# A hybrid attention and recurrence layer on one core: the first loads and transposes reordered, and a sixth token tile turned by VectorE and DRAM

## The chip, the core and the metric

The kernel runs on one core of one Trainium2 chip. A core has TensorE (matrix products and transposes, into PSUM banks of 128 x 512 f32), VectorE, ScalarE, GpSimd, and SyncE, which issues most DMAs. Each engine works through its own instructions in order and waits on semaphores for the others. The metric is the time of one execution on the device, in microseconds (us); lower is better. All data is f32, and no product may lose f32 accuracy.

## What is computed

One layer on 1024 tokens of width 1024, with 16 learned meta tokens ahead of them:

```python
h = concatenate([meta, x])                       # 1040 x 1024
u = rmsnorm(h, g_pre_mix);  z = u @ w_in         # -> q | k | v | x_rec | y_rec
attn = sliding_window_attention_with_sinks(q, k, v, sinks)   # 8 heads, window 128
xr = causal_depthwise_conv(x_rec, conv_w, conv_b)
rec = gelu(y_rec) * rg_lru(xr, w_a, b_a, w_x, b_x, lru_lambda)
h = h + rmsnorm(concatenate([attn, rec]) @ w_out, g_post_mix)
u = rmsnorm(h, g_pre_ffn)
f = square(relu(u @ w_ff1)) @ w_ff2
out = (h + rmsnorm(f, g_post_ffn))[16:]
```

`rmsnorm(x, g)` is x times the inverse root of (mean of x squared + 1e-6), times g.

## The kernel before, in words

**Products.** Every operand is split into a high part (rounded to fp32r) and a low part (the rest), and each f32 product is three fp32r products: high x high, high x low, low x high (`mm3`, L123; `part`, L279, does one of the three over all eight chunks of the contraction). ScalarE makes high parts (`nc.scalar.copy` or `activation`), VectorE the low parts. The engines' order is set by a scheduler that runs through the program with its own estimate of times; `behind(name, ins)` (L106) adds an order without a semaphore, `chained(e, ins)` (L332) strings instructions of ScalarE (e = 0) or VectorE (e = 1) together in the order of the text, and `lut` (L81) does so for ScalarE's table functions.

**The head** (up to about 50 us). SyncE issues the loads: meta, token tiles x0 and x1 (128 x 1024 each), the gains g_pre_mix and g_pre_ffn, then the columns of w_in for the keys, values and the first queries, further token tiles in between. The tokens go through in four blocks, `ALL` (L288): 272 columns (meta, x0, x1), then three of 256. For a block, `normed` (L320) makes the rows u without the gain: the square's sum on ScalarE, the inverse root (for x0 and x1 with ScalarE's Sqrt and VectorE's reciprocal, `norm_first` L232 and `root_rstd` L195; for the others with GpSimd's add and power, `norm_rows` L251 and `rstd_of` L167), and the scaling of the rows on VectorE. `transposed` (L351) then turns each of the eight 128-column chunks on TensorE into a PSUM bank (tags `pt`, `o`, `s`, two banks each), from where ScalarE writes the high part times the gain g_mix (L117) and VectorE the low part (L118). While this goes on, TensorE runs products of zeros: `load` (L307), 18 before the first transposes and one behind each chunk of block 0 (L365). The cast of the keys' weights stands in two halves between ScalarE's first evictions (`key_casts`, L344 and L368). Block 0's products are written out by hand (L503 to L525): keys and values in three parts, while x2 and x3 are normed, then two pairs of query heads. Blocks 1 to 3 (L526 to L530) are straight. The squares of x4 and of later tiles stand where the scheduler puts them.

**The middle** (to about 246 us) is attention, the convolutions and the recurrence, with projections filled in between on TensorE. It ends with the mix `at` = [attention | recurrence], ready in halves of 512 tokens.

**The output projection** (about 246 to 313 us). For each of the eight tiles t of 128 tokens, `out_mm` (L1030) makes two PSUM banks of 512 columns; `out_norm` (L1048) squares them on ScalarE (L1055), takes the inverse root on GpSimd (L172, L176), multiplies by root and g_post_mix on VectorE (L1061), adds x (L1064), stores h to `out` and squares h (L1067). h lies in a buffer of tag `raw`, of which there are two, shared with the loads of the feed-forward weights. `out_scale` (L1074) then brings the normed row tile into columns, in one of two ways. For t < `MOVED` (five tiles), `u2_store` (L1010) multiplies h by root and g_pre_ffn on VectorE with a dealt order of columns (L1011: every fourth column together), turns blocks of 32 x 32 on VectorE (L1018), and stores the result to DRAM, from where `u2_read` (L1021) fetches it with tokens along the columns. For the others ScalarE (t = 7: VectorE) scales the rows (L1081, L1079), and `u2_tiles` (L1087) turns them in eight TensorE transposes (L1093), with eight evictions that multiply by g_ffn (L1110 and L1101).

**The feed-forward products** (313 us to the end) are two Strassen-like schemes, over W1 and W2. The first sums of the token operand are made by `t_sums` (L1246) as tiles 4 to 7 come in.

Of the kernel before, what the change touches and what calls it, by code (L numbers as in the profile page):

```python
# [9 lines left out]
F32 = mybir.dt.float32  # L10
# [27 lines left out]
def hybrid_layer(  # L38
# [30 lines left out]
    def f32(ap):  # L69
        return ap.bitcast(F32)  # L70
# [68 lines left out]
    make_identity(nc, ident)  # L139

    meta_t = slot("d", [NMETA, D])
    nc.sync.dma_start(meta_t, meta_tokens)
    xt = []

    def load_x(i):
# [5 lines left out]
    load_x(1)  # L151

    vmt = const.tile([P, P], F32, name="vmt")
    g_r = vmt[0:16, :]
    nc.sync.dma_start(g_r[0:8, :], g_pre_mix.rearrange("o (k p) -> (o k) p", p=P))
    nc.sync.dma_start(g_r[8:16, :], g_pre_ffn.rearrange("o (k p) -> (o k) p", p=P))

    gcol = const.tile([P, 16], F32, name="gcol")
    pg = bank("o")
    nc.tensor.transpose(pg[:, :16], g_r, ident[:16, :16])  # L160
    nc.vector.tensor_copy(gcol, pg[:, :16])
    g_mix_col, g_ffn_col = gcol[:, 0:8], gcol[:, 8:16]

    half_pow = const.tile([P, 1], F32, name="half_pow")
# [27 lines left out]

    load_root()

    def root_rstd(ssq, bias, n=P):  # L195
        sd = small.tile([P, 1], F32, name="sd", tag="sd")
        lut(sd[:n], ssq, AF.Sqrt, bias=bias)
        rs = small.tile([P, 1], F32, name="rs", tag="rs")
        nc.vector.reciprocal(rs[:n], sd[:n])
        return rs[:n]  # L200


    def load_cols(cols, tag="ws"):
# [28 lines left out]
    def norm_first(src, halves):  # L232

        xn = slot("d", [P, D])
        ss = [small.tile([P, 1], F32, name=f"hq{i}", tag=f"hq{i}") for i in range(2)]
        c = slice(0, 512 if halves else D)
        nc.scalar.activation(
            xn[:, c], src[:, c], AF.Square, scale=RMS_SC, accum_out=ss[0]
        )
# [6 lines left out]
        rs = root_rstd(ss[0], ss[1] if halves else eps_col)  # L246
        for c in (slice(0, 512), slice(512, D)):
            nc.vector.tensor_scalar(xn[:, c], src[:, c], rs, None, op0=ALU.mult)
        return xn

    def norm_rows(src, n, link=False):  # L251
        xn = slot("d", [P, D])
        ssq = small.tile([P, 1], F32, name="ssq", tag="ssq")
        ins = nc.scalar.activation(
            xn[:n], src, AF.Square, scale=RMS_SC, accum_out=ssq[:n]
        ).ins
        if link:
            chained(0, ins)
        rs = rstd_of([ssq[:n]], n)
        ins = nc.vector.tensor_scalar(xn[:n], src, rs, None, op0=ALU.mult).ins  # L260
        if link:
            chained(1, ins)
        return xn

    def project(w, pieces, sink, after=None):
# [33 lines left out]

    zeros = slot("ws", [P, 512], F32R)  # L300
    nc.vector.memset(f32(zeros), 0.0)

    flip = [0]

# [9 lines left out]
                behind(after, ins)  # L314
        return ins.name

    load(12, 512)
    load(6, 256)

    def normed(b):  # L320
        if b == 0:
            return [
                (norm_rows(meta_t[:NMETA], NMETA), NMETA),
                (norm_first(xt[0], True), P), (norm_first(xt[1], False), P),
            ]
        rows = [(xt[2 * b], P), (xt[2 * b + 1], P)]
        return [(norm_rows(s[:m], m), m) for s, m in rows]


    last = [None, None]  # L330
# [3 lines left out]
            behind(last[e], ins)  # L334
        last[e] = ins.name

    def high_w(raw, tag="ws", parts=None):
        hi, lo = pair(tag, [P, KC, P])
        if parts is None:
            chained(0, nc.scalar.copy(hi, raw).ins)  # L340
            return hi, lo
        for ks in (slice(0, KC // 2), slice(KC // 2, KC)):
            parts.append(
                lambda ks=ks: chained(0, nc.scalar.copy(hi[:, ks], raw[:, ks]).ins)  # L344
            )
        return hi, lo

    def low_w(w, raw):
# [2 lines left out]
    def transposed(b, xn, after=None):  # L351
        t0, n = ALL[b]
        for kc in range(KC):
            flip[0] += 1
            pt = bank(("pt", "o", "s")[flip[0] % 3])
            o = 0
            for s, m in xn:
                ins = nc.tensor.transpose(
                    pt[:, o : o + m], s[:m, kc * P : (kc + 1) * P], ident[:m, :m]
                )  # L360
                if after:
                    behind(after, ins.ins)
                o += m
            if b == 0:
                load(1, P, ins.ins.name)  # L365
            uh, ul = u[kc]
            if b == 0 and kc in (0, 1):
                key_casts.pop(0)()  # L368
# [4 lines left out]
            if b == 0:  # L373
                chained(0, high[0])
                chained(1, high[1])

    def fetch(cols, tag="raw", pieces=1):
        raw = slot(tag, [P, KC, P])
# [21 lines left out]
    rq1 = fetch([(Q_COL + HD, HD), (Q_COL + 5 * HD, HD)], "e")  # L400
    for i in range(4, 8):
        load_x(i)
    key_casts = []
    wk = high_w(rk, "b", key_casts)
    transposed(0, xn)
    low_w(wk, rk)
    wv = high_w(rv, "b")
    low_w(wv, rv)
    wq = high_w(rq)
    low_w(wq, rq)  # L410
    km = slot("ws", [P, 4, 2 * P], F32R)
    nc.gpsimd.memset(f32(km[:, 0:2, 0 : P - NMETA]), 0.0)
    nc.gpsimd.memset(f32(km[:, 2:4, :]), 0.0)
    nsink = const.tile([P, 8], F32, name="nsink")
    nc.sync.dma_start(nsink, attn_sinks[0].partition_broadcast(P))
    prm_r = slot("d", [8, 512])
    nc.sync.dma_start(prm_r[0:4, :], conv_w[0])
    for i, src in ((4, conv_b), (7, lru_lambda)):
        nc.sync.dma_start(prm_r[i : i + 1, :], src)

    for i, src in enumerate((b_a, b_x)):
        for s in range(2):
            nc.sync.dma_start(
                prm_r[5 + s : 6 + s, :].rearrange("o (c t k) -> t o c k", t=2, k=HD)[i ^ s],
                src.rearrange("o (c t k) -> t o c k", t=2, k=HD)[s],
            )

# [71 lines left out]
    for b in range(4):  # L499
# [3 lines left out]
        if b == 0:  # L503

            acc = [bank("acc"), bank("acc")]
            for a, w in zip(acc, (wk, wv)):
                part(a, w, piece, 0)
                part(a, w, piece, 1)
            xn = [(norm_rows(xt[2], P, True), P)]
            xn.append((norm_rows(xt[3], P, True), P))  # L510
            part(acc[0], wk, piece, 2)
            sink_k(acc[0][:, : piece[1]], *piece)
            part(acc[1], wv, piece, 2)
            sink_v(acc[1][:, : piece[1]], *piece)
            wq1 = high_w(rq1)
            low_w(wq1, rq1)
            for w, (t0, n), sink, tag in (
                (wq, (16, 256), sink_q0, "o"), (wq1, (16, 256), sink_q1, "acc"),
            ):
                acc = bank(tag)  # L520
                for k in range(3):
                    part(acc, w, (t0, n), k)
                sink(acc[:, :n], t0, n)
            done.append(last_mm[0])
            continue  # L525
# [12 lines left out]
    pp = bank("o")  # L538
    for c in range(NLRU):
        nc.tensor.transpose(  # L540
            pp[:, c * 8 : (c + 1) * 8], prm_r[:, c * P : (c + 1) * P], ident[:8, :8]
        )
    nc.vector.tensor_copy(prm.rearrange("p a b -> p (a b)"), pp[:, :32])

    nc.vector.tensor_scalar(nsink, nsink, -1.0, None, op0=ALU.mult)

# [457 lines left out]
    gpre_b = slot("ws", [P, D])  # L1004
    nc.scalar.dma_start(gpre_b, g_pre_ffn[0].partition_broadcast(P))

    def dealt(t_):
        return t_.rearrange("p (n b) -> p b n", b=4)

    def u2_store(t, h, rs, tmp):  # L1010
        ins = nc.vector.scalar_tensor_tensor(  # L1011
            tmp.rearrange("p (b n) -> p b n", b=4), dealt(h), rs,
            dealt(gpre_b), op0=ALU.mult, op1=ALU.mult,
        ).ins
        if t < 3:
            behind(summed[t + 1], ins)
        y = slot("e", [P, D])
# [30 lines left out]
    def out_norm(t, po):  # L1048
# [3 lines left out]
        ssq = [small.tile([P, 1], F32, name=f"sq{n}", tag=f"sq{n}") for n in range(2)]  # L1052
        for n in range(2):
            c = slice(512 * n, 512 * n + 512)
            nc.scalar.activation(  # L1055
                h[:, c], po[n], AF.Square, scale=RMS_SC, accum_out=ssq[n]
            )
        rs = rstd_of(ssq)
        for n in range(2):
            c = slice(512 * n, 512 * n + 512)  # L1060
            nc.vector.scalar_tensor_tensor(  # L1061
                h[:, c], po[n], rs, gmix_b[:, c], op0=ALU.mult, op1=ALU.mult
            )
# [590 lines left out]
```

## Time and profile before

| | |
|---|---|
| time, median of 3 runs (lowest, highest) | 946.97 us (946.8, 948.84) |
| the profiled execution: its time, its span | 947.39 us, 945.6 us |
| TensorE busy, matmuls | 936.1 us, 4576 |
| VectorE, ScalarE, GpSimd busy | 663.6, 506.4, 134.1 us |
| moved by DMA, mean rate | 135.96 MB, 144 GB/s |

The span runs from the first to the last instruction of the program; the execution's time has some two us more around it. Verdicts compare times of the whole execution. In the profile PE is TensorE, PEld its loading of weights, DVE is VectorE, ACT is ScalarE, POOL is GpSimd, SP is SyncE; a q behind the name is an engine's queue, which waits and issues. L12 is line 12 of the kernel before. A line of the timeline has start, duration, engine, line, operation, tiles written and read, shapes and a count, and in brackets the idle time ahead of it with what ended it. Matmuls are pipelined, so the duration of one (0.39 us for 512 columns) is longer than the distance to the next. The mean granted TensorE clock of the profiled execution is 0.998.

### The profile page before, as it was taken

The numbers are of one execution on the slowest core, as the hardware profiler recorded it, in microseconds if no ns is written. First come the engines' busy times: TensorE is split into PE (matmuls) and PEld (weight loads), VectorE is DVE, ScalarE is ACT, GpSimd is POOL, SyncE is SP. The second block draws the span as 40 slices with busy tenths as digits, with TensorE's granted clock in tenths as the row PEclk, the third lists the DMA queues.
The fourth block names the chain that finished last, engine by engine and source line by source line (L and its number), as shares of the span: only waits on it lengthen the run. The fifth ranks groups of instructions, "written<-read, shape, count | busy, mean of one in ns | idle before, by whom it ended". The sixth has DMA issues, their size and how long they took to land.

```text
span 945.6 us, 12176 instructions
## 1 busy us (share of the span) xinstructions
PE 936.1 (99%) x4576; PEld 783.4 (83%) x4576; DVE 663.6 (70%) x843; ACT 506.4 (54%) x847; POOL 134.1 (14%) x205
## 2 busy tenths in 40 slices
PE   9999999999999999999999999999999999999996
PEld 8999999877888888888888888888888888888885
DVE  6667788889977986755544465476667676779883
ACT  7546766579534864443655575654533443445441
POOL 4104436421021100110000000001111000001201
PEclk9999999999999999999999999999999999999999
DMA  9221011104259768574422364334787756547924
GB/s 273 58 52 39 24 46 40 51 23 134 93 186 299 222 196 281 184 251 135 156 89 89 113 217 120 107 112 113 199 170 172 213 179 193 187 133 208 242 62 89
DMA packets 99623, 135.96 MB, mean 144 GB/s; under 512 B 24359, under 2 KB 63287, under 8 KB 99565
## 3 DMA queue, kind: packets, MB, share of 16 engines
q1 hardware_dynamic: 90252, 109.69, 36.6%
q0 software_dynamic: 8880, 24.19, 12.1%
q10 hardware_dynamic: 432, 1.31, 0.4%
q8 instruction: 36, 0.59, 0.3%
q14 instruction: 23, 0.18, 0.1%
HBM read 113.08 MB, written 21.50 MB: 142 GB/s over the span
## 4 chain that ended last, share of the span: by engine, by line
PE 98%; DVE 1%; issue 0%; ACT 0%; DVEq 0%
PE ps_acc L125 11%; PE ps_acc L131 11%; PE ps_acc L130 11%; PE ps_pt L130 7%; PE ps_pt L125 7%; PE ps_pt L131 7%; PE ps_s L125 6%; PE ps_s L131 6%; PE ps_s L130 6%; PE ps_o L125 5%; PE ps_o L130 5%; PE ps_o L131 5%; PE ps_o L699 2%; PE ps_acc L924 1%; PE ps_s L629 1%; PE ps_s L633 1%
## 5 line engine op out<-in xcount | busy, mean ns | idle before, releaser
L99 DVE TENSOR_TENSOR ws<-raw,ws 128x1024 fp32r<-128x1024 f32 (+1 forms) x69 | 83.1, 1204 | 73.1 <-ACT ws L96 23.6
L96 ACT CAST ws<-raw 128x1024 fp32r<-128x1024 f32 (+1 forms) x68 | 69.7, 1026 | 83.1 <-PE ps_o L130 33.1
L96 ACT CAST ws<-e 128x1024 fp32r<-128x1024 f32 x41 | 43.0, 1049 | 85.1 <-PE ps_o L130 37.8
L99 DVE TENSOR_TENSOR b<-b,b 128x1024 fp32r<-128x1024 f32 (+1 forms) x49 | 57.5, 1176 | 27.6 <-PE ps_o L130 22.3
L130 PE MATMUL ps_acc<-a,ws 128*128 128x512 f32 (+3 forms) x224 | 76.3, 341 | 0.0
L125 PE MATMUL ps_acc<-a,ws 128*128 128x512 f32 (+3 forms) x224 | 76.3, 341 | 0.0
L131 PE MATMUL ps_acc<-a,ws 128*128 128x512 f32 (+3 forms) x224 | 75.7, 338 | 0.0
L96 ACT CAST b<-b 128x1024 fp32r<-128x1024 f32 (+1 forms) x49 | 49.5, 1011 | 41.7 <-DVE b L1124 35.5
L99 DVE TENSOR_TENSOR ws<-e,ws 128x1024 fp32r<-128x1024 f32 x41 | 50.1, 1222 | 29.6 <-ACT ws L96 16.6
L686 POOL TENSOR_SCALAR_AFFINE_SELECT c<-c 128x512 fp32r<-128x512 f32 x64 | 53.1, 845 | 73.6 <-ACT c L96 64.6
L131 PE MATMUL ps_acc<-ws,b 128*128 128x512 f32 (+1 forms) x120 | 46.1, 384 | 0.0
L130 PE MATMUL ps_acc<-ws,b 128*128 128x512 f32 (+1 forms) x120 | 46.1, 384 | 0.0
L125 PE MATMUL ps_acc<-ws,b 128*128 128x512 f32 (+1 forms) x120 | 46.0, 385 | 0.0
L125 PEld LDWEIGHTS ps_acc<-a,ws 128*128 128x128 f32 x224 | 42.2, 188 | 3.1 <-DVE b L933 0.3
L131 PEld LDWEIGHTS ps_acc<-a,ws 128*128 128x128 f32 x224 | 42.2, 188 | 3.0
L130 PEld LDWEIGHTS ps_acc<-a,ws 128*128 128x128 f32 x224 | 42.1, 188 | 2.8
L125 PE MATMUL ps_pt<-ws,b 128*128 128x512 f32 x112 | 44.2, 395 | 0.0
L130 PE MATMUL ps_pt<-ws,b 128*128 128x512 f32 x112 | 44.2, 394 | 0.0
L131 PE MATMUL ps_pt<-ws,b 128*128 128x512 f32 x112 | 44.0, 393 | 0.0
L125 PE MATMUL ps_s<-ws,b 128*128 128x512 f32 x110 | 43.5, 395 | 0.0
L130 PE MATMUL ps_s<-ws,b 128*128 128x512 f32 x110 | 43.3, 393 | 0.0
L131 PE MATMUL ps_s<-ws,b 128*128 128x512 f32 x110 | 43.2, 393 | 0.0
(423 smaller groups left out, 2682.8 us busy)
## 6 DMA issues: line engine op xcount, KB each, us to landing
raw<-in_w_ff_dram SPq DMA_DIRECT2D x59, 512.0 KB, 4.0
e<-in_w_ff_dram SPq DMA_DIRECT2D x43, 512.0 KB, 3.4
a<-in_w_ff_dram SPq DMA_DIRECT2D x12, 512.0 KB, 5.6
s_dram<-a POOLq DMA_DIRECT2D x12, 512.0 KB, 3.9
raw<-in_w_in_dram SPq DMA_DIRECT2D x9, 512.0 KB, 3.8
c<-in_x_dram SPq DMA_DIRECT2D x8, 512.0 KB, 5.3
d<-in_x_dram SPq DMA_DIRECT2D x8, 512.0 KB, 3.4
out_dram<-raw SPq DMA_DIRECT2D x8, 512.0 KB
```

The source lines that it names most:

```text
L96: cast[0] = nc.scalar.copy(hi, src).ins.name
L99: low = nc.vector.tensor_tensor(lo, src, f32(hi), op=ALU.subtract).ins
L125: ins = nc.tensor.matmul(dst, lh, rh, start=start, stop=False, skip_group_check=True).ins
L130: nc.tensor.matmul(dst, lh, rl, start=False, stop=False, skip_group_check=True)
L131: last_mm[0] = nc.tensor.matmul(dst, ll, rh, start=False, stop=stop, skip_group_check=True).ins.name
L629: nc.tensor.matmul(dst, q[h][:, c], hi, start=True, stop=False, skip_group_check=True,)
L633: nc.tensor.matmul(dst, q[h][:, c], lo, start=False, stop=True, skip_group_check=True,)
L686: nc.gpsimd.affine_select(out=p_[:, :, s], in_=f32(p_[:, :, 0]), pattern=[[0, 4], [g, P]], compare_op=op, fill=0.0, base=0, channel_multip ...
L699: nc.tensor.matmul(two[:, :, oc : oc + w], v, p_.rearrange("p (j i) s c -> p j (i s c)", j=2)[:, :, pc : pc + w], start=n == 0 and k == 0, ...
L924: ins = nc.tensor.matmul(y2_bank[half], (wh, wh, wl)[k][:, kc, :], (uh, ul, uh)[k][:, t0 : t0 + n], start=m % 24 == 0, stop=m % 24 == 23, ...
```

## The change

In the head:

- meta is issued on ScalarE's DMA queue, so that x0 and x1 are first on SyncE's. g_pre_ffn is no longer loaded there; it comes with the small parameters later (`prm_r` is 8 x 640 now) and is turned with them.
- 11 products of zeros instead of 18, and none between the chunks of block 0.
- Of the keys' cast, ScalarE does the first half ahead of its evictions, VectorE the second half behind the scaling of x1.
- VectorE scales x0, then meta (`norm_meta`), then x1; the square of x1 is put behind x0's root on ScalarE.
- `transposed_first` writes block 0's transposes out in order: x0's for six chunks, g_mix, meta's for six chunks, then x1's chunk by chunk. The copy of g_mix goes to ScalarE.
- In block 2 the squares of x4 and x5 are chained behind ScalarE's earlier casts, and the scalings of every later block stand behind the low part of the block before; the negation of the sinks stands behind the scaling of x5.

In the output projection:

- `MOVED` is 6: tile 5 too goes over VectorE and DRAM.
- In `u2_store` ScalarE deals the columns and multiplies by the root, and VectorE multiplies by g_pre_ffn, which ScalarE has dealt once beforehand (`gpre_n` to `gpre_b`).
- In `out_norm` VectorE multiplies the bank by g_post_mix first, ScalarE squares the bank in place, and one VectorE operation multiplies by the root and adds x.

```diff
-    nc.sync.dma_start(meta_t, meta_tokens)
+    nc.scalar.dma_start(meta_t, meta_tokens)
...
-    nc.sync.dma_start(g_r[8:16, :], g_pre_ffn.rearrange("o (k p) -> (o k) p", p=P))
...
-    load(12, 512)
-    load(6, 256)
+    load(11, 512)
...
+            xm, scale = norm_meta()
+            first = norm_first(xt[0], True)
+            scale()
+            return [(xm, NMETA), (first, P), (norm_first(xt[1], False), P)]
+        after = mark[0]
+        rows = [(norm_rows(xt[2 * b + i], b == 2, after), P) for i in range(2)]
...
+    wk = pair("b", [P, KC, P])
+    chained(0, nc.scalar.copy(wk[0][:, 0:4], rk[:, 0:4]).ins)
+    last[1] = scaled[0]
+    chained(1, nc.vector.tensor_copy(wk[0][:, 4:8], rk[:, 4:8]).ins)
+    transposed_first(xn)
...
+        for kc in range(6):
+            pts.append(bank(("o", "s", "pt")[kc % 3]))
+            turn(pts[kc][:, NMETA : NMETA + P], xa[:, cols(kc)])
+        pg = bank("acc")
+        turn(pg[:, :8], g_r)
+        chained(0, nc.scalar.copy(g_mix_col, pg[:, :8]).ins)
+        for kc in range(6):
+            turn(pts[kc][:, :NMETA], xm[:NMETA, cols(kc)])
...
-    MOVED = 5
+    MOVED = 6
...
+    nc.scalar.copy(gpre_b.rearrange("p (b n) -> p b n", b=4), dealt(gpre_n))
...
-        ins = nc.vector.scalar_tensor_tensor(
-            tmp.rearrange("p (b n) -> p b n", b=4), dealt(h), rs,
-            dealt(gpre_b), op0=ALU.mult, op1=ALU.mult,
-        ).ins
+        nc.scalar.activation(
+            tmp.rearrange("p (b n) -> p b n", b=4), dealt(h), AF.Copy, scale=rs
+        )
+        ins = nc.vector.tensor_tensor(tmp, tmp, gpre_b, op=ALU.mult).ins
...
+            nc.vector.tensor_tensor(h[:, c], po[n], gmix_b[:, c], op=ALU.mult)
             nc.scalar.activation(
-                h[:, c], po[n], AF.Square, scale=RMS_SC, accum_out=ssq[n]
+                po[n], po[n], AF.Square, scale=RMS_SC, accum_out=ssq[n]
             )
         rs = rstd_of(ssq)
-            nc.vector.scalar_tensor_tensor(
-                h[:, c], po[n], rs, gmix_b[:, c], op0=ALU.mult, op1=ALU.mult
-            )
-        summed[t] = nc.vector.tensor_tensor(h, h, xr, op=ALU.add).ins.name
+        summed[t] = nc.vector.scalar_tensor_tensor(
+            h, h, rs, xr, op0=ALU.mult, op1=ALU.add
+        ).ins.name
```

More of the change, by code (lines that the diff above doesn't have):

```diff
@@ L236, in norm_first @@
         c = slice(0, 512 if halves else D)
-        nc.scalar.activation(
+        square = nc.scalar.activation(
             xn[:, c], src[:, c], AF.Square, scale=RMS_SC, accum_out=ss[0]
-        )
+        ).ins
+        if not halves:
+            behind(last_lut[0], square)
         if halves:
@@ L254, in norm_rows @@
         ins = nc.scalar.activation(
[L255 removed]
+            xn, src, AF.Square, scale=RMS_SC, accum_out=ssq
         ).ins
@@ L258, in norm_rows @@
             chained(0, ins)
[L259 to L262, printed above, removed]
+        rs = rstd_of([ssq])
+        ins = [nc.vector.tensor_scalar(xn, src, rs, None, op0=ALU.mult).ins]
+        if after:
+            behind(after, *ins)
+        elif link:
+            for i in ins:
+                chained(1, i)
+        scaled[0] = ins[0].name
         return xn
@@ L315, in load @@
         return ins.name
-    load(12, 512)
-    load(6, 256)
+    load(11, 512)
     def normed(b):
         if b == 0:
[L322 to L327, printed above, removed]
+            xm, scale = norm_meta()
[4 more added lines that the diff above has]
+        rows = [(norm_rows(xt[2 * b + i], b == 2, after), P) for i in range(2)]
+        scaled.append(scaled[0])
+        return rows
     last = [None, None]
@@ L335, in chained, with high_w @@
         last[e] = ins.name
-    def high_w(raw, tag="ws", parts=None):
+    def high_w(raw, tag="ws"):
         hi, lo = pair(tag, [P, KC, P])
[L339 to L345, printed above, removed]
+        chained(0, nc.scalar.copy(hi, raw).ins)
         return hi, lo
```

115 lines of the change are left out of this document (77 added, 38 removed).

## The prediction

> **What bounds the kernel now.** I read the page first: the span, the engines' busy time, and the chain that ended last.
>
> ```profile
> span 945.6 us, 12176 instructions
> ...
> PE 936.1 (99%) x4576; PEld 783.4 (83%) x4576; DVE 663.6 (70%) x843; ACT 506.4 (54%) x847; POOL 134.1 (14%) x205
> ...
> PE 98%; DVE 1%; issue 0%; ACT 0%; DVEq 0%
> ```
>
> TensorE is the bound: it is on 98% of the chain. So a change can gain in three ways only: fewer TensorE instructions, an earlier first useful product, or a TensorE wait removed. Next I asked for TensorE's waits over the whole span; these three lines are the whole answer (waiting line, what released it, us, times, longest).
>
> ```profile
> PE ps_acc L309 <- DVE base_e L563: 1.5, 1, 1.5
> PE ps_acc L282 <- ACT ws L340: 0.6, 1, 0.6
> PE ps_acc L125 <- DVE b L480: 0.2, 1, 0.2
> ```
>
> The first is the start; the rows of the other two, at 22.91 and 28.86, follow below. So the head is where the change can find idle time. Everywhere else TensorE is dense and only removed instructions count. The timeline of the head (start, duration, engine, line) gives the rest:
>
> ```profile
> 0.80 0.40 SPq L142 DMA_DIRECT2D d<-in_meta_tokens_dram  x1
> ...
> 1.26 0.88 SPq L147 DMA_DIRECT2D c<-in_x_dram  x2
> ...
> 1.51 6.44 PE L309 MATMUL ps_acc<-ws 128*128 128x512 f32 x18 [1.51 <-DVE base_e L563]
> ...
> 5.66 0.74 DVE L260 TENSOR_SCALAR d<-d,rs 16x1024 f32<-16x1024 f32 x1
> ...
> 6.36 1.06 ACT L237 ACTIVATE d<-c 128x1024 f32<-128x1024 f32 x1 [0.22 <-DMA c<-in_x_dram]
> 6.50 0.88 DVE L248 TENSOR_SCALAR d<-c,rs 128x512 f32<-128x512 f32 x2
> ...
> 8.07 0.91 DVE L248 TENSOR_SCALAR d<-c,rs 128x512 f32<-128x512 f32 x2
> ...
> 9.27 0.49 ACT L117 ACTIVATE a<-ps_o,gcol 128x272 fp32r<-128x272 f32 x1 [0.93 <-PE ps_o L358]
> ...
> 9.66 0.61 ACT L344 CAST b<-raw 128x512 fp32r<-128x512 f32 x1
> ...
> 10.16 0.49 ACT L117 ACTIVATE a<-ps_s,gcol 128x272 fp32r<-128x272 f32 x1
> ...
> 12.24 5.13 PE L282 MATMUL ps_acc<-a,b 128*128 128x272 f32 x37
> ...
> 12.40 0.53 ACT L117 ACTIVATE a<-ps_s,gcol 128x272 fp32r<-128x272 f32 x1
> ```
>
> Dense work begins with the group at 12.24, paced by the last of ScalarE's eight first-block evictions (L117), which starts at 12.40. They follow each other every 0.37 us (10.16 to 12.40, the second to the eighth), except that the keys' cast (9.66) puts the second 0.89 us behind the first.
>
> **The change part by part: the head.** (1) x0 takes meta's place on SP: its issue moves from 1.26 to 0.80, 0.46 us. I take the same for the landing of x1, on which ScalarE waited at 6.36. Bounds: 0, if bandwidth and not issue sets the landing, and 0.46. meta's issue (0.40) now stands on ScalarE's queue ahead of its table load; ScalarE waits for x afterwards, which covers it. One small load (g_pre_ffn, 4 KB) leaves the head; it is needed only at the out-projection.
>
> (2) VectorE scales x0 (0.88), meta (0.74), x1 (0.91). meta stood ahead of x0 and now stands between x0 and x1: the sum until x1 is scaled stays 2.5 us, and moves by the 0.46 at most.
>
> (3) Half of the keys' cast leaves ScalarE: of the 0.89 us between the first two evictions 0.5 go. VectorE gets it behind x1's scaling, where it waited for the first eviction (8.07 + 0.91 to 9.27 + 0.49). That wait is the cover; without it the cast would cost at most its 0.61 us.
>
> (4) x0's transposes go first, then g_mix and meta, while x1 is still being scaled; the eight filler matmuls between the blocks go. Behind x1's first scaled half one transpose per block is left. The first eviction began 1.20 us behind the start of that scaling (8.07 to 9.27); I take 0.85, so 0.35 less, bounds 0 and 0.6. The copy of g_mix moves to ScalarE, below 0.49 (an eviction of 272 columns; this one has 8), and is covered by the 0.93 us that ScalarE waited at 9.27.
>
> Sum at the start of the dense work: 0.46 + 0.5 + 0.35 = 1.3 us; with (1) and (4) at their low bounds 0.5. I take 1.1.
>
> (5) The other two waits of TensorE:
>
> ```profile
> 20.35 1.06 ACT L254 ACTIVATE d<-c 128x1024 f32<-128x1024 f32 x1 [1.62 <-DMA c<-in_x_dram]
> ...
> 21.81 1.05 ACT L340 CAST ws<-e 128x1024 fp32r<-128x1024 f32 x1
> ...
> 22.89 1.23 DVE L349 TENSOR_TENSOR ws<-e,ws 128x1024 fp32r<-128x1024 f32 x1 [1.40 <-ACT ws L340]
> 22.91 3.11 PE L282 MATMUL ps_acc<-a,ws 128*128 128x256 f32 x24 [0.62 <-ACT ws L340]
> ...
> 24.03 0.75 DVE L260 TENSOR_SCALAR d<-c,rs 128x1024 f32<-128x1024 f32 x1
> ...
> 28.86 0.36 PE L125 MATMUL ps_acc<-a,b 128*128 128x256 f32 x1 [0.20 <-DVE b L480]
> ```
>
> ScalarE stood 1.62 us for the landing of x4, from 18.73 on, with the copy of v and the cast of the second query weights (21.81) queued behind it. TensorE then waited for that cast, and VectorE, late with its low parts, gave the third wait. The new order chains x4's square behind that cast and puts x4's scaling (24.03) behind the second block's low parts. The cast can then start near 19.5, and is done about two us before TensorE came to it (22.91 - 0.62 = 22.29). Both waits, 0.8 us, go, and what stood around them: the first of the three waits set VectorE back by its 1.40 us, so low parts paced TensorE until the row at 28.86. I take 1.1 us, bounds 0.6 and 1.5. Late next is VectorE, with the scalings of x4 and x5 (0.75 each); it has the 1.40 us to spend on them.
>
> **The sixth tile.** Eight transposes leave TensorE; a row of the chain of waits has the price of such a group:
>
> ```profile
> 313.42 0.87 PE ps_o L1093 x8
> ```
>
> I count 0.8 us, as a small transpose (g_ffn) comes in elsewhere. It holds only if nothing is late. First the operations of a stored tile (least, median, most ns), then the waits on them, then the timeline, then two stretches (TensorE, its loads, VectorE, ScalarE, GpSimd, clock, DMA share, GB/s):
>
> ```profile
> L1011 DVE SCALAR_TENSOR_TENSOR d<-raw,rs,ws x5: 2018/2077/2083, 270.3 to 295.0; 128x1024 f32<-128x1024 f32 x5
> ...
> L1061 DVE SCALAR_TENSOR_TENSOR raw<-ps_acc,rs,e x4: 743/747/751, 274.5 to 300.0; 128x512 f32<-128x512 f32 x4
> ...
> L1018 DVE STREAM_TRANSPOSE e<-d x5: 1236/1245/1246, 272.4 to 301.9; 128x1024 f32<-128x1024 f32 x5
> ...
> L1081 ACT ACTIVATE d<-raw,rs x2: 1152/1152/1153, 304.2 to 318.7; 128x1024 f32<-128x1024 f32 x2
> ```
>
> ```profile
> ACT raw L1055 <- DVE d L1011: 2.7, 3, 1.0
> ```
>
> ```profile
> 297.17 0.60 ACT L1055 ACTIVATE raw<-ps_acc 128x512 f32<-128x512 f32 x1 [0.74 <-DVE d L1011]
> ...
> 313.89 2.18 ACT L1110 ACTIVATE c<-ps_o,gcol 128x128 f32<-128x128 f32 x8 [1.72 <-PE ps_o L1093]
> ...
> 316.18 0.68 DVE L1124 TENSOR_TENSOR a<-c,c 128x512 f32<-128x512 f32 x1
> ```
>
> ```profile
> 280.00:291.00 11.00, 11.00 (x49) 8.95 (x48) 9.41 (x11) 3.07 (x9) 2.47 (x4) 1.00 0.97 305
> ...
> 313.00:325.00 12.00, 12.00 (x60) 9.89 (x59) 11.12 (x15) 10.08 (x24) 2.94 (x5) 1.00 0.78 243
> ```
>
> VectorE's share of a stored tile was 2 x 0.75 (L1061), 1.23 (the addition, by the row at 22.89), 2.08 (L1011) and 1.25 (L1018), 6.1 us. It becomes 2 x 0.7 (near L1124's 0.68), 1.23, 1.23 and 1.25, 5.1 us. ScalarE gets the dealing: the trace has no dealt ScalarE copy, so it lies between L1081's 1.15 and L1011's 2.08; I take 1.2, by the same operation undealt. ScalarE is busy 3.07 of 11 us there, so either is hidden. The `raw` buffer of a tile, for which the squares waited on L1011, comes free when ScalarE has dealt, one long VectorE operation earlier, and the multiplication by g_post_mix no longer waits for the root. So tile 5 should start ahead of its old 297.17. It must be back by 316.18, when t_sums reads it. In exchange ScalarE loses 2.18 us of evictions just ahead of tile 7's squares, where it is busy 10.08 of 12 us. I book nothing for that: TensorE has no wait there.
>
> The dealt copy of g_pre_ffn, once 1.2 to 2.1 us, is hidden if ScalarE makes it in its wait here:
>
> ```profile
> 250.38 0.62 ACT L96 CAST b<-b 128x512 fp32r<-128x512 f32 x1 [6.11 <-DVE b L885]
> ...
> 235.00:245.00 10.00, 10.00 (x45) 7.91 (x44) 10.00 (x10) 9.26 (x15) 0.00 (x0) 1.00 0.33 107
> ```
>
> In the 6.11 us it is free; earlier, where VectorE is busy 10.00 of 10 us and ScalarE feeds it, it could cost its whole length. I take 0.
>
> Sum: 1.1 + 1.1 + 0.8 = 3.0 us. The profiled execution took 947.39 us (its span and 1.8 around it), 0.4 above the median of the three runs shown, 946.97; taken from the median the sum gives 944.0.
>
> **Rivals.** A. *TensorE is slow when the dense work starts.*
>
> ```profile
> 1.50:6.80 5.30, 5.29 (x12) 4.13 (x13) 1.00 0.88 272
> ```
>
> Twelve 512-column matmuls took 5.3 us, 0.44 each; from 280 to 291, 49 of that size took 11.0, 0.22 each. So TensorE starts at half speed (the clock column says 1.00 and doesn't show it), and was fast by 12.24, where 37 products of 272 columns took 5.13 us. The change ends its warming matmuls after eleven, near 1.51 + 11 x 0.44 = 6.4, and takes out the fillers; until the dense work only transposes and single products follow. If it is slow then, and needs again the 5.3 us or more of work, it loses half of that, 2.6 us; I give the rival 1.2 to 2.6, middle 1.9: 945.9. Against it: the transposes and products from 6.4 on may keep it fast. [...]
>
> B. *The head moves less.* x1 lands no earlier, and VectorE stays late in the second block: 0.5 + 0.6 + 0.8 = 1.9, which gives 945.1; the dealt copy in the crowded stretch gives about the same, 3.0 - 1.2 = 1.8.
>
> C. *Slower: tile 5 comes back late.* At the old pace the stores' transposes came every 7.4 us (272.4 to 301.9 for five), so the sixth at 309.3, done at 310.5. What follows, by the medians from issue to landing:
>
> ```profile
> s_dram<-a POOLq DMA_DIRECT2D x12, 512.0 KB, 3.9
> ...
> c<-u_dram SPq DMA_DIRECT2D x20, 128.0 KB, 3.6
> ```
>
> A store like the first, 3.9, four reads, 3.6 and about 2 for their issue: 320. The change adds 1 MB to DMA, which is at 0.97 and 305 GB/s from 280 to 291: up to 3.4 us more, 323.4. That is 4 to 7 us behind 316.18, middle 5.6. VectorE works 11.12 of 12 us there, in order, so it can't make this good, and TensorE's next products need t_sums: 949.6. It ends slower from some 5 us late on. Against it: the shorter hold of `raw` and VectorE's shorter tile.
>
> **Chances.** Forecast 0.53 (its own range 942.4 to 945.0), A 0.24, B 0.12, C 0.11. About 0.2%, 1.9 us, is what a measurement of this kernel can tell from no change; on the fast side that line is 945.1. The forecast lies below it, with half of B: faster 0.59, same 0.30, slower 0.11. The range leaves C out. Down it takes the high bounds (1.3 + 1.5 + 0.9 = 3.7, and 0.9 for an order of instructions that I can't see), up the upper ends of A and B: 942.4 to 947.0.
>
> **What would show it.** Right: L117 evictions evenly 0.37 us apart, the last starting near 11.3; no wait of TensorE on L340 or L480; two groups of eight output transposes instead of three. Wrong: first products that take twice their time behind the last eviction (A); ScalarE still waiting for x1 past 6.2 (B); VectorE idle on the reads of tile 5 ahead of t_sums (C); or new TensorE waits behind 30 us, where I expect none.

## The result, and the profile after

| | before | after |
|---|---|---|
| median of 6 runs (lowest, highest), us | 946.61 (946.35, 948.84) | 953.33 (952.44, 953.81) |
| ratio to before, 95% interval | | 1.0065 [1.0055, 1.0075] |
| span of the profiled execution, us | 945.6 | 950.7 |

The change made the kernel 6.2 us slower by the ratio (6.7 by the medians); the prediction was 944.0, faster, with 942.4 to 947.0 as its range.

The page of after first: span, busy time, and the shares of the chain that ended last.

```profile
span 950.7 us, 12134 instructions
...
PE 935.7 (98%) x4554; PEld 781.5 (82%) x4554; DVE 660.2 (69%) x846; ACT 516.6 (54%) x845; POOL 132.5 (14%) x205
...
PE 94%; ACT 3%; DVE 1%; issue 1%; DMA 0%; POOL 0%; DVEq 0%; ACTq 0%; POOLq 0%
```

TensorE has 22 matmuls less and is busy 0.4 us less, but it is on 94% of the chain instead of 98%. So it waits now, and the view of its waits (waiting line, releaser, us in total, times, longest) says where:

```profile
PE ps_acc L125 <- ACT b L96: 4.0, 1, 4.0
PE ps_acc L339 <- DVE base_e L627: 1.5, 1, 1.5
PE ps_pt L125 <- ACT a L96: 1.5, 2, 0.8
PE ps_o L401 <- DVE d L248: 0.5, 1, 0.5
```

The waits in the head on the second query cast and on the low parts are gone, as forecast; the start (1.5) has stayed. New are 4.0 us in one piece and 1.5 us in two. The timeline has the 4.0 us (start, duration, engine, line; the bracket is the idle time ahead):

```profile
334.05 0.40 PE L131 MATMUL ps_pt<-b,a 128*128 128x512 f32 x1
338.48 0.57 PE L125 MATMUL ps_acc<-b,e 128*128 128x512 f32 x1 [4.04 <-ACT b L96]
339.05 0.79 PE L130 MATMUL ps_acc<-b,e 128*128 128x512 f32 x1
...
340.06 0.63 PE L125 MATMUL ps_acc<-b,e 128*128 128x512 f32 x1
340.49 0.63 PE L130 MATMUL ps_acc<-b,e 128*128 128x512 f32 x1
```

The product at 338.48 is the first that reads the sums over both token halves (`ot2`), so it needs every tile. In before it began at 335.35 without a wait:

```profile
335.35 0.39 PE L125 MATMUL ps_acc<-b,e 128*128 128x512 f32 x1
335.59 0.39 PE L130 MATMUL ps_acc<-b,e 128*128 128x512 f32 x1
```

The bracket in after names a cast of ScalarE, which itself waited for VectorE's sums; VectorE has no idle time in the whole wait (first line of run 6 below). Behind the wait the products follow each other in 0.43 us (340.06 to 340.49) instead of before's 0.23. The path of tile 5 to those sums, in the timelines of ScalarE, VectorE and SyncE:

```profile
302.23 2.11 ACT L1077 ACTIVATE d<-raw,rs 128x1024 f32<-128x1024 f32 x1 [0.98 <-POOL rs L172]
...
304.38 1.22 DVE L1080 TENSOR_TENSOR d<-d,ws 128x1024 f32<-128x1024 f32 x1 [3.16 <-ACT d L1077]
...
311.26 1.23 DVE L1084 STREAM_TRANSPOSE e<-d 128x1024 f32<-128x1024 f32 x1
...
312.52 0.33 SPq L1085 DMA_DIRECT2D u_dram<-e  x1
...
316.06 2.04 SPq L1089 DMA_DIRECT2D c<-u_dram  x3
...
320.41 0.69 DVE L1188 TENSOR_TENSOR a<-c,c 128x512 f32<-128x512 f32 x1 [2.27 <-DMA c<-u_dram]
```

Between the product with g_pre_ffn (304.38) and the transpose (311.26) VectorE does six other operations; the tile is stored at 312.52, and VectorE stands 2.27 us for its return. t_sums starts at 320.41, against 316.18 before.

### The profile page after: what moved, and what is told of

Same layout as the page of the kernel before. It is cut to its first block, busy times and chain, and to the rows that moved or that the text cites. A ratio compares the mean times of both kernels' runs of the same rounds, so it can differ in the third digit from the quotient of the medians.

```text
span 950.7 us, 12134 instructions
## 1 busy us (share of the span) xinstructions
PE 935.7 (98%) x4554; PEld 781.5 (82%) x4554; DVE 660.2 (69%) x846; ACT 516.6 (54%) x845; POOL 132.5 (14%) x205
## 4 chain that ended last, share of the span: by engine, by line
PE 94%; ACT 3%; DVE 1%; issue 1%; DMA 0%; POOL 0%; DVEq 0%; ACTq 0%; POOLq 0%
PE ps_acc L130 11%; PE ps_acc L125 11%; PE ps_acc L131 11%; PE ps_s L131 6%; PE ps_s L130 6%; PE ps_s L125 6%; PE ps_pt L125 6%; PE ps_pt L130 6%; PE ps_pt L131 6%; PE ps_o L130 5%; PE ps_o L125 5%; PE ps_o L131 5%; PE ps_o L763 2%; ACT c L82 1%; PE ps_acc L309 1%; PE ps_s L693 1%
## 5 line engine op out<-in xcount | busy, mean ns | idle before, releaser
L96 ACT CAST ws<-raw 128x1024 fp32r<-128x1024 f32 (+1 forms) x68 | 69.8, 1026 | 84.2 <-PE ps_o L130 33.1
L96 ACT CAST ws<-e 128x1024 fp32r<-128x1024 f32 x41 | 43.0, 1050 | 85.5 <-PE ps_o L130 38.4
L96 ACT CAST b<-b 128x1024 fp32r<-128x1024 f32 (+1 forms) x49 | 49.5, 1011 | 42.3 <-DVE b L1188 35.5
```

What stands on the lines that cost most here:

```text
L96: cast[0] = nc.scalar.copy(hi, src).ins.name
```

## The experiments

Times are medians; runs of before on the same chip stand beside each. Those medians were 945.74 for the first four runs, 947.36 for the next four and 946.3 for the last four, so kernels of different batches are compared by their ratios.

**1. The head alone**: after's head, and before's whole output stage (five stored tiles, dealt by VectorE).

> The head of the change alone, with the output projection as before (five tiles, VectorE deals, root ahead of the gain). Theory: the change's loss has three parts: the head gains about 1.9 us (TensorE reaches the 220 us mark that much earlier), ScalarE's dealt copy of g_pre_ffn in the crowded stretch gives 1.8 of it back (two waits of TensorE near 224 and 232 us), and tile 5 comes back late (a wait of 4.2 us near 334 us, and about 1.9 us of half speed behind it). Then this kernel takes 946.6 - 1.9 = 944.7 us. Rival: the gain of the head is lost later anyway, because VectorE's chain ahead of the output projection sets the pace: 946.6.

945.24 (before 945.74), ratio 0.9994 [0.9985, 1.0003]. Between the two: the head wins about half a microsecond, not 1.9, and the interval doesn't exclude nothing at all. What explains most of the gap came with run 12.

**2. The new output stage with five tiles.**

```diff
-    MOVED = 6
+    MOVED = 5
```

> The changed kernel with five tiles over DRAM again, all else as changed. Theory (the sixth tile is what costs): the wait near 334 us and the half speed go, the copy's cost stays: 946.6 - 1.9 + 1.8 = 946.5 us. Rival (the rebuilt chain costs: a dealt ScalarE copy of 2.15 us instead of 1.2, and the new order of the norm): the wait stays, 951 to 953.

947.07 (before 945.74), ratio 1.0012 [1.0003, 1.0021]: as the theory had it. The sixth tile costs the step from 1.0012 to 1.0065, 5.0 us; the rest of the output stage costs 1.7 us over the head alone.

**3. The sixth tile in the old output stage**: before with `MOVED = 6`, nothing else.

> The kernel before with the sixth tile alone. Theory: the sixth tile adds 2.08 + 1.25 us of VectorE work and a round trip through DRAM to a stretch in which VectorE is busy 97% and TensorE's product at 335 us starts as soon as its operand is made: a wait of 3 us or more there, 949 to 953. Rival (the rebuilt chain costs, not the tile): the eight transposes go and nothing is late, 945.8.

954.96 (before 945.74), ratio 1.0092 [1.0078, 1.0106]. The sixth tile costs 8.7 us there, more than expected; so the tile is dear without the new chain (ScalarE deals) too, and the new chain is the cheaper of the two.

**4. Tile 5 turned earlier**: `behind(stored[5], ...)` puts the first half's low parts, and tile 6's product with g_post_mix, behind tile 5's transpose.

> The changed kernel with one order added: VectorE turns tile 5 before the low parts of the first operand and before tile 6's product with the gain, 5 us earlier than it did. Theory: VectorE's wait of 2.3 us on the reads of tile 5 goes, but the 2.5 us of VectorE work of the sixth tile stay, so TensorE still waits about 2 us near 334 us, with or without half speed behind it: 949 to 951. Rival (only this order is at fault): the whole 6 us come back, 947.2.

952.49 (before 945.74), ratio 1.0067 [1.0055, 1.008]. Both expectations missed. The wait on the read went, and another took its place (VectorE's timeline of this run):

```profile
318.15 0.68 DVE L1192 TENSOR_TENSOR a<-c,c 128x512 f32<-128x512 f32 x1
...
324.09 0.16 DVE L168 SCALAR_TENSOR_TENSOR ms<-sq,sq 128x1 f32<-128x1 f32 x1 [2.12 <-ACT ps_pt L1126]
```

The sums start 2.3 us earlier (318.15), but then VectorE stands 2.12 us for the squares of tile 7, which ScalarE makes behind tile 6's scaling. So "tile 5 comes back late" alone wasn't the cause; the theory had to be split into what VectorE has to do and what it has to wait for.

**5. Five tiles, with the dealt copy of g_pre_ffn late.**

```diff
-    nc.scalar.copy(gpre_b..., dealt(gpre_n))
+    behind(wo_last, nc.scalar.copy(gpre_b..., dealt(gpre_n)).ins)
```

(`wo_last` is the last cast of w_out.)

> The kernel after with five stored tiles instead of six, and with the dealt copy of g_pre_ffn put behind the last cast of w_out on ScalarE, where ScalarE stood 6.11 us for VectorE before. The five-tile kernel with the copy in its old place gave 947.07 against 945.24 for the head alone. Theory: the 1.8 us are the copy's 2.05 us in a crowded stretch of ScalarE (TensorE's waits of 0.98 and 0.84 us near 224 and 232), so they go: 945.2, and no wait of TensorE on the casts of w_out. Rival: the 1.8 us belong to the new output stage, or the copy in its new place holds up the casts of the gated products: 947.

945.82 (before 947.36), ratio 0.9988 [0.9979, 0.9997]. The copy's cost is gone, and this version is the only one whose whole interval lies below 1. In after the copy stood here (ScalarE's timeline), in this kernel at 241.99:

```profile
215.50 2.05 ACT L1074 COPY ws<-e 128x1024 f32<-128x1024 f32 x1
```

```profile
241.99 2.07 ACT L1077 COPY ws<-e 128x1024 f32<-128x1024 f32 x1
...
248.22 0.62 ACT L96 CAST b<-b 128x512 fp32r<-128x512 f32 x1 [4.16 <-DVE b L949]
```

Of ScalarE's stand of 6.11 us 4.16 are left. The two waits of TensorE on the casts of w_out (1.5 us in after) don't occur.

**6. The wait of after filled** with 16 idle products: at p = 0 of the loop over p, TensorE makes 16 products of 512 columns, whose results nothing reads, ahead of the product with `ot2`.

> The kernel after with 16 idle products of 512 columns (3.7 us at 0.23) on TensorE in the wait ahead of the first product that reads the sums of the two token halves. Theory: the wait is filled, not shortened, that product still starts near 338.5, but the eight products behind it take 0.23 us instead of 0.43, because TensorE wasn't idle: 1.6 to 1.9 us less than after, 951.5. Rival: those products are slow for another reason (their weights, the transfers of that moment): no change, 953.3.

951.87 (before 947.36), ratio 1.0051 [1.0039, 1.0064], 0.14% under after's ratio: 1.3 us. The stretch behind the wait, in after and then here (TensorE busy and matmuls, its loads, VectorE, ScalarE, GpSimd, granted clock, DMA share, GB/s):

```profile
334.40:338.40 4.00, 0.04 (x1) 0.00 (x0) 4.00 (x10) 1.63 (x3) 0.65 (x1) 1.00 0.12 47
338.40:342.20 3.80, 3.72 (x9) 2.67 (x10) 3.66 (x6) 3.40 (x5) 0.00 (x0) 0.55 0.75 229
342.20:350.00 7.80, 7.80 (x35) 6.36 (x34) 7.45 (x13) 3.58 (x6) 1.08 (x2) 1.00 0.25 88
```

```profile
334.00:338.40 4.40, 3.94 (x17) 2.83 (x16) 4.40 (x11) 1.73 (x4) 0.65 (x1) 1.00 0.07 26
338.40:342.20 3.80, 3.47 (x14) 2.64 (x15) 3.66 (x7) 3.50 (x6) 0.00 (x0) 1.00 0.94 268
```

With idle products the granted clock stays at 1.00 and 14 products fit where 9 did at 0.55. The transfers of that moment weren't the cause: there are more of them here (0.94 against 0.75).

**7. The read of tile 5 not waiting for its store.**

```diff
-                u2_dram[t, :, :, 64 * q : 64 * q + 64]...
+                u2_dram[min(t, 4), :, :, 64 * q : 64 * q + 64]...
```

> The kernel after, where the read of tile 5 fetches the place of tile 4, so that it doesn't wait for the store of tile 5 (its tokens are then wrong; every instruction is still made). Theory, since the run that turned tile 5 earlier won only 0.8 us: VectorE's wait of 2.27 us on that read goes, but 0.7 of it come back in the wait for the squares of tile 7 on ScalarE, so 1.6 us less than after, 951.7, with the wait ahead of the sums' product near 2.4 us and the half speed still there. Rival: the late read is the whole cost of the sixth tile: 947 to 948. Second rival: VectorE's own queue sets it, and nothing changes: 953.

951.45 (before 947.36), ratio 1.0046 [1.0032, 1.006], 1.8 us under after: the theory. The product with `ot2` comes at

```profile
337.48 0.50 PE L125 MATMUL ps_acc<-b,e 128*128 128x512 f32 x1 [2.95 <-ACT b L96]
```

1.0 us earlier than in after, and still 2.65 us later than in run 2 (334.83). With the read no longer waiting for the store, those 2.65 us were left to explain, near the 2.45 us of VectorE's two operations for it (1.22 and 1.23). The run is still 4.4 us slower than before, so the late read isn't the whole cost.

**8. Tile 5 without VectorE's two operations**, dealt by ScalarE straight into the stored buffer.

> The kernel after, where tile 5 is dealt by ScalarE straight into the buffer that is stored: VectorE's product with g_pre_ffn (1.23) and its transpose (1.24) are left out for this tile alone (its tokens are then wrong). Theory: VectorE's two operations and the 3.16 us that it stands for ScalarE's dealing ahead of them are the cost of the sixth tile, since everything that the sums' product needs stands behind them on VectorE. Without them that product starts as with five tiles (334.8), without a wait over 1 us: 946 to 948. Rival: what holds it is ScalarE's dealing, the order of ScalarE's work for tiles 6 and 7, or the transfers: above 951.

957.46 (before 947.36), ratio 1.0106 [1.0092, 1.012]: slower, and inconclusive. With other instructions the scheduler wrote another order. ScalarE dealt tile 5 six microseconds later, and VectorE then stood 6.63 us for a cast that ScalarE had behind other work:

```profile
308.30 2.16 ACT L1078 ACTIVATE e<-raw,rs 128x1024 f32<-128x1024 f32 x1
...
317.72 1.04 ACT L96 CAST b<-raw 128x1024 fp32r<-128x1024 f32 x1
...
318.79 1.22 DVE L99 TENSOR_TENSOR e<-raw,b 128x1024 fp32r<-128x1024 f32 x1 [6.63 <-ACT b L96]
```

The suspected work had to be added instead of taken away:

**9. VectorE's two operations alone**, on top of run 5 (five tiles).

```diff
+        if t == 5:
+            y = slot("e", [P, D])
+            nc.vector.tensor_tensor(y, h, gpre_b, op=ALU.mult)
+            nc.vector.transpose(y, gpre_b)
```

> The kernel with five stored tiles and the late copy (945.82 beside 947.36 for before), to which only VectorE's two operations of the sixth tile are added: a product of 128x1024 and a 32x32 transpose of 128x1024 into a spare buffer, nothing of which is read; tile 5 still goes through TensorE's transposes. Theory: these 2.46 us of VectorE are the larger part of the sixth tile's cost, because all that the sums' product needs stands behind them on VectorE. That product starts 1 to 2.5 us later (333.2 before), TensorE waits for it, and the time rises by 1.2 to 3 us: 947 to 949. Rival: they fit into the waits that VectorE has there (3.1 near 302, 0.9 near 318, 1.0 near 322): at most 946.3, and no new wait of TensorE.

948.96 (before 946.3), ratio 1.0026 [1.0015, 1.0037], against 0.9988 without them: 3.6 us for 2.45 us of work. That the work costs time is the theory's; the size is a little above what it expected. The product in run 5, here, and two stretches behind it here (the columns as in run 6):

```profile
333.21 0.39 PE L125 MATMUL ps_acc<-b,e 128*128 128x512 f32 x1
```

```profile
335.67 0.50 PE L125 MATMUL ps_acc<-b,e 128*128 128x512 f32 x1 [2.43 <-ACT b L96]
```

```profile
335.60:336.90 1.30, 1.23 (x4) 0.86 (x5) 1.25 (x3) 1.30 (x4) 0.00 (x0) 1.00 0.00 0
336.90:340.30 3.40, 3.40 (x9) 2.65 (x8) 3.40 (x5) 2.02 (x3) 0.00 (x0) 0.50 0.00 0
```

The product starts 2.46 us later, about as long as the work. That the two lengths agree isn't proof that VectorE absorbed nothing: in this execution a load of feed-forward weights landed late, well before the added work,

```profile
293.20 1.05 ACT L96 CAST a<-raw 128x1024 fp32r<-128x1024 f32 x1 [1.64 <-DMA raw<-in_w_ff_dram]
```

and VectorE came to tile 5's addition at 298.28 instead of 296.83, with 1.45 us of delay that isn't the work's. What rests on seven executions is the 3.6 us. Behind the wait the clock is at 0.50 for 3.4 us: the twelve products with `ot2` take 4.67 us (335.67 to 340.34) instead of 2.77 in run 5.

**10. Work taken off VectorE in after**: GpSimd makes the two low parts of `b21`.

> The kernel after with six stored tiles, where the two low parts of the second half's operand (128x1024 each, 2.35 us of VectorE ahead of tile 5's transpose and beside it) are made by GpSimd. Theory: VectorE's queue is what holds the sums' product back, so with 2.35 us less on it ahead of the sums that product starts 1.5 to 2.4 us earlier (338.5 in after), and the time falls by as much: 951 to 952. Rival: VectorE only waits longer for the read of tile 5 and for ScalarE, or GpSimd's slower low parts hold up the products that read them near 324: no change or slower, 953.3 or more.

954.85 (before 946.3), ratio 1.0091 [1.0076, 1.0106]: the rival, slower. GpSimd's rows and VectorE's beside them:

```profile
308.33 5.76 POOL L1198 TENSOR_TENSOR b<-c,b 128x1024 fp32r<-128x1024 f32 x2 [6.02 <-ACT b L1197]
```

```profile
309.11 2.71 DVE L1198 TENSOR_TENSOR b<-c,b 128x1024 fp32r<-128x1024 f32 x1
...
312.90 1.20 DVE L168 SCALAR_TENSOR_TENSOR ms<-sq,sq 128x1 f32<-128x1 f32 x1
```

VectorE's low part took 2.71 us instead of 1.22, and the addition of two columns 1.20 instead of 0.14; the latter ends at 314.10, with GpSimd (308.33 + 5.76). So VectorE got back all of the 2.35 us taken off it. The product with `ot2` starts at 337.41, 1.1 us earlier than in after (half of that comes from the head, whose end is at 54.23 there and at 54.75 in after), but behind it TensorE stands 1.55 us more for a low part, and the clock is at 0.50 for 6.7 us. The run neither confirms the theory nor speaks against it, and shows that this relief isn't one.

**11. The late copy with six tiles** (run 5's edit on after).

> The kernel after with six stored tiles, and the dealt copy of g_pre_ffn behind the last cast of w_out. With five tiles this brought the copy's 1.8 us back. Theory: it does here too, since the out-projection paces what follows, so that the sums' product also comes 1.8 us earlier: 951.5 (a ratio near 1.0046 instead of 1.0065). Rival: what TensorE wins is only a longer wait ahead of the sums' product, whose chain on VectorE hasn't moved: no change, 953.3.

951.37 (before 946.3), ratio 1.005 [1.0036, 1.0064], 1.4 us under after: the theory. The long wait is still 4.0 us, and the product behind it starts at 336.50, 2.0 us earlier than in after. Not all of that arrives at the end, because the slow stretch is longer here (the end of the wait, and the twelve products behind it; the columns as in run 6):

```profile
334.90:336.50 1.60, 0.00 (x1) 0.00 (x1) 1.60 (x5) 0.40 (x1) 0.52 (x1) 0.50 0.36 141
336.50:341.70 5.20, 5.20 (x12) 3.95 (x13) 5.06 (x9) 3.38 (x5) 0.00 (x0) 0.50 0.53 160
```

The clock was at 0.50 before TensorE resumed, and stayed there for 6.8 us in all; after had 3.4 us of it behind a wait of the same length.

**12. Before once more**, for a second profile.

> The kernel before once more, for a second profile of its head. Theory: its profile had an execution that was 1.2 us late in the head (the first attention product at 56.72; at 55.48 in the kernel whose head is the same and whose output stage alone differs), so this one starts that product near 55.5 and spans some 944.4. Rival: the kernel's head always runs so: 56.7 and 945.6.

945.55, span 943.8: the theory. Its waits of TensorE are

```profile
PE ps_acc L309 <- DVE base_e L563: 1.5, 1, 1.5
PE ps_o L358 <- DVE d L248: 0.6, 1, 0.6
```

and x4's square and the second query cast stand at

```profile
18.61 1.07 ACT L254 ACTIVATE d<-c 128x1024 f32<-128x1024 f32 x1
...
20.07 1.05 ACT L340 CAST ws<-e 128x1024 fp32r<-128x1024 f32 x1
```

without the 1.62 us of waiting for x4, and without TensorE's waits on L340 and L480. So x4's late landing belongs to that execution and not to every one; run 3, with the same head, doesn't show these waits either. How often x4 lands late, three profiles don't say: of the 15 executions of before that stand beside runs 5 to 8, eight took 947.3 us or more and seven 946.6 or less, and whether the longer ones are those isn't shown.

## Why the prediction was wrong, step by step

By the ratios of runs 1 and 2 and of after the 6.2 us are: head -0.6, output stage with five tiles +1.7, sixth tile +5.0 (each with 1 to 1.4 us of uncertainty). The prediction had -2.2, 0 and -0.8. What gave the wrong sign is the last. It is where rival C, which the prediction gave 0.11, expected it, but only part of it is C's mechanism.

**The sixth tile: its path was followed to its start, not to its return, and VectorE's work for it was left out of the sum.** The step that failed is "It holds only if nothing is late": the forecast let tile 5 start ahead of 297.17, took that for enough to be back by 316.18, and booked nothing for VectorE's two operations for it. Tile 5 did start earlier (its first square at 296.63), and yet came back at 320.41, 4.2 us late. On its path, ScalarE's dealing was taken at 1.2 us and measured 2.11, near the upper bound of 2.08. VectorE's 3.16 us of waiting for it are not new, though: before it stood as long in the same place, for a cast:

```profile
306.32 1.23 DVE L99 TENSOR_TENSOR ws<-raw,ws 128x1024 fp32r<-128x1024 f32 x1 [3.20 <-ACT ws L96]
```

New are the product with g_pre_ffn, the 5.66 us from its end to the transpose, in which VectorE works through other rows (304.38 + 1.22 to 311.26), and the store and read back. VectorE's shorter operations were summed (6.1 to 5.1 us a tile), but the sum that mattered was another: the sixth tile adds 2.45 us of VectorE work ahead of the sums, which five tiles leave to TensorE and ScalarE, in a stretch where the prediction itself had read 11.12 busy of 12 us.

The profiled executions of run 2 and of after show where the 5.0 us lie. The product with `ot2` starts 3.65 us later (338.48 in after; in run 2 the line below), and from it to the end 612.2 us pass instead of 610.4; together 5.5. The eight transposes that leave TensorE, +0.8 in the forecast, gained nothing: TensorE came to that product 0.54 us earlier (the last one ahead of it at 334.05, in run 2 at 334.59), and that became wait, because VectorE's queue set the start. Of the 3.65 us run 7 takes off 1.0 with the wait on the read (1.8 us of the time), and 2.65 are left for VectorE's work; run 9 puts that work at 3.6 us of the time, its own slow stretch included. The sizes of the two shares aren't exact: in the profile of run 7, as in that of run 9, a load landed late and tile 5's addition stood 1.3 us later than in after (300.05, 298.78). Run 4 shows why repairing the order alone won nothing: behind the read stood the next wait.

```profile
334.83 0.39 PE L125 MATMUL ps_acc<-b,e 128*128 128x512 f32 x1
```

**The clock: 1.3 to 1.9 us that no rival had at this place.** The prediction used the half speed of TensorE in the head only (rival A). Where the dense work starts it wasn't seen: in after the first three transposes of x0 followed each other at 0.22 to 0.23 us (7.08 to 7.53), those from 7.71 on at 0.11, as in before's groups of eight (0.87 us at 313.42), and the 34 products of 272 columns from 11.92 took 4.75 us, 0.14 each (before: 37 in 5.13). In after the half speed came behind the new wait: the twelve products with `ot2` take 4.65 us in after (338.48 to 343.13) and 2.78 in before (335.35 to 338.13), 1.9 us more; run 6 brought 1.3 of the time back. The stretches at 0.50 (0.51 in run 7) lasted 3.4 us in runs 9, 7 and after, and 6.8 us in run 11, and a wait of 2.43 us was enough for one (run 9). What sets their length, no run shows.

**The dealt copy: "I take 0".** Its length was in the upper bound (2.05; bounds 1.2 to 2.1), its place was the bad one of the two that the prediction named: 215.50, in the stretch where ScalarE feeds VectorE, and not in the 6.11 us of waiting near 246. The prediction left the place to the scheduler instead of asking where its inputs allow it: the gain is loaded long before, so it is ready early, and nothing held it back. It cost some 2 us (run 5 against run 2: 0.9988 and 1.0012), and 1.4 us in after (run 11), where the longer slow stretch took back a part.

**The head: 2.2 us forecast, 0.6 to 0.7 found.** The removal of TensorE's two waits (1.1 us, with "bounds 0.6 and 1.5") was read from an execution in which x4 landed late; in run 12 they don't exist. So the step removed something that only some executions have, and 0 should have been its low bound. The other 1.1 us were nearer. The first attention product, the end of the head, starts in before's two profiles and in five_late's at (first and last start of its group)

```profile
L629 PE MATMUL ps_s<-ws,b x8: 277/280/364, 56.7 to 136.3; 128*128 128x256 f32 x8
```

```profile
L629 PE MATMUL ps_s<-ws,b x8: 278/280/366, 55.2 to 134.8; 128*128 128x256 f32 x8
```

```profile
L693 PE MATMUL ps_s<-ws,b x8: 277/280/362, 54.5 to 134.1; 128*128 128x256 f32 x8
```

that is 0.7 us earlier than in the second profile of before, and 2.2 earlier than in the one from which the prediction was made. Step by step, in after: the evictions do follow evenly, so the keys' half cast gave what was taken for it; the first begins at 9.11 instead of 9.27, and the last at 11.71, where 11.3 was forecast. Of the 1.3 us summed for it, step (3) gave its 0.5, step (4) 0.17 of 0.35 (from the start of x1's scaling, 8.08, to the first eviction, 9.11, are 1.03 us; 1.20 before, 0.85 forecast), and step (1) nothing:

```profile
4.12 1.06 ACT L260 ACTIVATE d<-d 16x1024 f32<-16x1024 f32 x1 [1.38 <-DMA d<-in_meta_tokens_dram]
...
4.83 0.69 DVE L242 CUSTOM_DVE_ANT_0 d<-c 128x512 f32<-128x512 f32 x1 [3.36 <-DMA c<-in_x_dram]
...
8.08 0.91 DVE L248 TENSOR_SCALAR d<-c,rs 128x512 f32<-128x512 f32 x2
```

x0 lands 0.21 us earlier (4.83, before 5.04), not 0.46, and x1's scaling starts at 8.08 as before (8.07). meta, moved to ScalarE's queue, lands later (its square starts at 4.12, before 2.98), and that square, which stands ahead of x0's on ScalarE, ends only at 5.18, when x0 had been there for 0.35 us. In the head-only run x0 was there at 4.42 and x1's scaling began at 7.79, so step (1) is worth 0 to 0.3 us at x1, depending on how the loads land.

**What held.** The two groups of eight transposes instead of three, no wait on the second query cast or the low parts, the even evictions, and the place of rival C: VectorE idle on the read of tile 5 ahead of t_sums. Its lateness, 5.6 us, was near the 4.2 found, in part by luck: the transpose came 2.0 us later than C's 309.3, and the way through DRAM was shorter (312.52 to 320.41, 7.9 us) than C's 9.5 to 12.9. C counted the whole lateness of the read as cost, of which run 7 gives back 1.8 us, and didn't count VectorE's own work for the tile, the clock or the copy.

**Open**: why the sixth tile costs 8.7 us in the old output stage (run 3) and 5.0 in the new one wasn't tested. By the traces the difference lies behind the product with `ot2`. In run 3 that product starts 282.5 us behind the first attention product, in before 278.6: 3.8 us later, as in the new stage. But from it to the end 615.4 us pass, 610.3 in before, with another wait of 0.94 us and the clock at 0.50 for 6.8 us. Open too is how the 3.65 us divide exactly between VectorE's work and the read.

## What to carry to other kernels

When work moves from the bounding engine to one that is off the path, follow the moved item to the instruction that consumes it, with each engine's whole queue in order between, and count the added work against the spare time of the receiving engine in that stretch, not its busy share of the whole span. Take a second profile before a wait of a fraction of a microsecond on a load becomes a term of the sum. And give a one-time preparation a place (behind a named instruction, in a measured gap), or it goes where its inputs are ready.

## What the runs showed of the hardware

- A wait of TensorE can cost more than itself. Behind 2.43, 2.95 and 4.04 us of waiting (runs 9, 7 and after) came 3.4 us at a granted clock of 0.50 (0.51 in run 7), and twelve products took 4.65 to 4.67 us instead of 2.8: 1.9 us lost each time. In runs 9 and 7 the clock was still at 1.00 when TensorE resumed, and the slow stretch began about 1.2 us later. The length of the wait doesn't set the loss alone: in run 11, also behind 4.04 us, the slow stretch began within the wait and lasted 6.8 us, and the twelve products took 5.34 us. Two waits below 1 us in after (0.82 ahead of 225.43, 0.68 ahead of 232.88) had no such tail: the clock is at 1.00 from 223 to 236.
- ScalarE's dealt operations of 128x1024 (every fourth f32 read) took 2.05 to 2.16 us. Its undealt scaling of rows of that size took 1.15 (before, L1081), a plain cast 1.05 (L96).
- While GpSimd's two low parts ran in run 10 (308.33 to 314.09), two of VectorE's operations took longer: 2.71 us (1.22 for the same operation ahead of them, at 306.77), and 1.20 (0.14 in after). The second ends together with GpSimd's (312.90 + 1.20, 308.33 + 5.76). The transpose between them (311.74) took 1.23 us, as in after. What sets these apart, no run shows.
